# Moving the low weight halves by 64 bytes, and the first layer's mixer from three narrow products a block to a wide and a narrow one

## The chip, the cores and the metric

The kernel runs on one core of a Trainium2 chip. Its engines work side by side, each through a queue of its own: TensorE (PE; its weight loads are listed as PEld), VectorE (DVE), ScalarE (ACT), GpSimd (POOL) and SyncE (SP), which here issues the DMAs. The metric is the device time of one execution in microseconds.

## The reference

Two layers over one sequence of 256 tokens with 2,048 features, in float32. In each layer:

- from the vector `c`, 6 x 2,048 modulation values (a product with `ada_w`, 2,048 x 12,288);
- a root-mean-square norm of x with modulation, then one input projection `w_in` (2,048 x 8,704) into queries, keys and values of two attentions (A: a window of 128 tokens with grouped keys; B: a neighbourhood on a grid 64 wide, with a bias table) and two gates of 2,048 columns;
- each attention's output is projected (`w_proj_a`, `w_proj_b`, 1,024 x 2,048), multiplied by the sigmoid of its gate, and the sum goes through `w_out` (2,048 x 2,048) and is added to x;
- a second modulated norm, `w_up` (2,048 x 11,264), a depthwise convolution of width 3 over the tokens, SiLU of one half times the other half, `w_down` (5,632 x 2,048), added to x.

```
h = rmsnorm(x, norm_mix[l]) * (1.0 + sc_a) + sh_a
qa, ka, va, qb, kb, vb, ga, gb = split_cols(h @ w_in[l])
...
merged = jax.nn.sigmoid(ga) * ya + jax.nn.sigmoid(gb) * yb
x = x + gt_a * (merged @ w_out[l])
```

## The kernel before

**Blocks and units.** All weight matrices are cut into blocks of 128 x 128. A layer has 232 units of 16 blocks, in the order in which they are used (`block_stream`, L69). A unit is one DMA of 1 MB into a `raw` tile (four buffers, shared with the modulation weights `aw`, each 1 MB as well). `unit` (L216) splits each half of it, 8 blocks, into two float32r tiles: ScalarE copies the rounded value, *hi* (L225), and VectorE subtracts it from the original, *lo* (L226). Both lie in one tile `hl` of 128 x 2 x 1,024 elements, lo 4,096 bytes after hi in each partition; there are four such buffers, two units.

**Products.** The activations are split in the same way: `h[:, kc, 0]` is the high half, `h[:, kc, 1]` the low one, 256 tokens each, side by side. A product is the sum of three: hi with high, hi with low, lo with high.

- *Features* (`feature_run`, L230): a weight block stands in the array, the activations stream through. In the *joint* form there are three products of 256 columns a block, all into the same half of a PSUM bank (L239 to L241). In the other form there is a *wide* one of 512 columns, hi with both halves of the activations (L248 or L253), into both halves of the bank, and a *narrow* one of 256, lo with the high half (L250). A run has the blocks of half a unit: in a first run the wide products come first and then the narrow ones, in a later run the narrow ones and then the wide ones. The two halves of the bank have then to be added: `sum_halves` (L344) is a ScalarE copy of one (L346) and a VectorE addition of the other (L347).
- *Tokens* (`tokens`, L326): for queries, keys and values the activations stand in the array and four weight blocks stream (L337 to L339), 512 columns each.

**Stages of a layer**, in order: token products for q, k, v; gate A (`gate_a`); projection A (`proj_a`); gate B (`gate_b`); projection B (`merge`); out-projection (`out_evac`, with `residual`); then three times an up-projection with its convolution and a down-projection (`down`). Layer 0 works its token products and gate A in four parts of the contraction, with gate A always joint. `JOINT` (L49) says for proj_a, gate_b, merge and the out-projection whether they are joint: in layer 0 they are, in layer 1 not. `whole` (L738) gives the evacuation the bank's half where it is joint, and a tile `z` with the sum of halves where it isn't; `residual` (L782) takes one VectorE operation a column where joint, and two where not. The last column (from `ENDING` = 15) of an out-projection and of the last down-projection is joint in both layers.

**What sets the order.** The code is written in the order of the weight stream. Between units `Stream.tick` runs background work: `Paced` (L176) advances the attention heads by a rate a tick, and `plan` (L165) issues modulation products (L162, VectorE) so that a given number is done at a given unit (`ADA_PLAN_0`, `ADA_PLAN_1`); three quarters of them fall into layer 0. SP issues the DMAs in order and waits for a free `raw` buffer, which VectorE gives back. PSUM has four banks for these products (`mm`) and three for the rest (`ax`).

**Where the tiles lie.** Pools are laid out in the order in which they are made: `const` (with x), `lay`, `raw`, `hl`, `h` (h and merged share one place), `ev`, `at`, `sm`, and `s`, which holds ya, the packed q, k, v, oA, oB and the activations between up- and down-projection. oA's heads 6 and 7 lie in `ev`. In bytes of a partition: hl from 70,688, h from 103,456, ev's tiles for oA 6 and 7 from 140,320, s from 163,296; a tile's place is rounded up to 32 bytes.

Of the kernel before, what the change touches and what calls it, by code (L numbers as in the profile page):

```python
# [9 lines left out]
F32 = mybir.dt.float32  # L10
F32R = mybir.dt.float32r
AF = mybir.ActivationFunctionType
ALU = mybir.AluOpType
AX = mybir.AxisListType

P = 128
L = 2
# [16 lines left out]
GATE_A, GATE_B = 4608, 6656  # L34
# [11 lines left out]
ADA_PLAN_0 = [(38, 32), (58, 48), (76, 66), (84, 70), (96, 80), (128, 96), (145, 108), (175, 118), (192, 124), (230, 143)]  # L46
ADA_PLAN_1 = [(0, 143), (76, 169), (84, 165), (95, 176), (129, 192)]

JOINT = [True, False]  # L49

FIRST_RATE = 0.65
ENDING = 15
# [16 lines left out]
def block_stream(l):  # L69

    seq = []
    for part in K_PARTS[l]:
        for g in QKV_GROUPS:
            for kc in part:
                seq += [("w_in", kc, g // P + j) for j in range(4)]
        for mo in range(KC):
            seq += [("w_in", kc, GATE_A // P + mo) for kc in part]
    for mo in range(KC):
        seq += [("w_proj_a", kc, mo) for kc in range(HA)]
    for mo in range(KC):  # L80
        seq += [("w_in", kc, GATE_B // P + mo) for kc in range(KC)]
    for mo in range(KC):
        seq += [("w_proj_b", kc, mo) for kc in range(HB)]
    for mos in OUT_TURNS:
        seq += [("w_out", kc, mo) for kc in range(KC) for mo in mos]
    for gi, chunks in enumerate(FF_GROUPS):
        cols = [c + h * FC for c in chunks for h in range(2)]
        if gi == 0:
            for kc in range(KC):
                seq += [("w_up", kc, m) for m in cols[:4]]  # L90
            cols = cols[4:]
        for m in cols:
            seq += [("w_up", kc, m) for kc in range(KC)]
        for mos in OUT_TURNS:
            seq += [("w_down", kc, mo) for kc in chunks for mo in mos]
    return seq


UB = 16
NU = len(block_stream(0)) // UB  # L100
NA = len(ADA_ORDER)


# [1 line left out]
def encoder(ctx: ExitStack, tc: tile.TileContext, a: dict, out: bass.AP):  # L105
    nc = tc.nc
    pool = lambda name, bufs, **kw: ctx.enter_context(tc.tile_pool(name=name, bufs=bufs, **kw))
    const = pool("const", 1)
    lay = pool("lay", 2)
    rawp = pool("raw", 4)  # L110
    hlp = pool("hl", 4)
    hp = pool("h", 1)
    ev = pool("ev", 3)
    at = pool("at", 2)
    sm = pool("sm", 3)
# [19 lines left out]

    cact = const.tile([P, D], F32, name="cact")
    nc.sync.dma_start(cact[:1], a["c"])
    one = sm.tile([1, P], F32, name="one", tag="one", bufs=1)
    nc.vector.memset(one[:], 1.0)
    for i in range(0, D, 512):  # L140
        cb = ax.tile([P, 512], F32, name="cb", tag="ax")
        nc.tensor.matmul(cb[:], one[:], cact[:1, i : i + 512], start=True, stop=True)
        nc.scalar.activation(out=cact[:, i : i + 512], in_=cb[:], func=AF.Silu)
    x = const.tile([P, KC, S], F32, name="x")
    sp = pool("s", 1)

    def place(tag, n, dt, name):
# [67 lines left out]

    def unit(l, u):  # L216

        raw = rawp.tile([P, UB * P], F32, name=f"w{l}_{u}", tag="raw")
        nc.sync.dma_start(raw[:], a["ws"][l, u])
        halves = []  # L220
        for j in range(2):
            n = UB * P // 2
            hl = hlp.tile([P, 2, n], F32R, name=f"hl{l}_{u}_{j}", tag="hl")
            r = raw[:, j * n : (j + 1) * n]
            nc.scalar.copy(hl[:, 0], r)  # L225
            nc.vector.tensor_tensor(out=hl[:, 1], in0=r, in1=hl[:, 0].bitcast(F32), op=ALU.subtract)  # L226
            halves.append(hl)
        return halves

    def feature_run(run, joint):  # L230

        wide, narrow = [], []
        for ps, hl, j, act, first, last in run:
            hi, lo = hl[:, 0, j * P : (j + 1) * P], hl[:, 1, j * P : (j + 1) * P]
            out = ps[:].rearrange("p (a s) -> p a s", a=2)
            if joint:
                nc.tensor.matmul(out[:, 0], hi, act[:, 0], start=first, stop=False)  # L239
                nc.tensor.matmul(out[:, 0], hi, act[:, 1], start=False, stop=False)  # L240
                nc.tensor.matmul(out[:, 0], lo, act[:, 0], start=False, stop=last)  # L241
                continue
            wide.append((out, hi, act, first, last))
            narrow.append((out[:, 0], lo, act[:, 0]))
        begins = any(w[3] for w in wide)
        for o, w, act, first, last in wide:
            if begins and not last:
                nc.tensor.matmul(o, w, act, start=first, stop=False)  # L248
        for o, w, act in narrow:
            nc.tensor.matmul(o, w, act, start=False, stop=False)  # L250
        for o, w, act, first, last in wide:
            if last or not begins:
                nc.tensor.matmul(o, w, act, start=False, stop=last)  # L253

    class Stream:
# [16 lines left out]
        def prefetch(self, n):  # L272

            for _ in range(n):
                self.ahead.append(unit(self.l, self.u + len(self.ahead)))
# [13 lines left out]
        def next_block(self):  # L289
            if self.at == UB:  # L290
                if self.ahead:
                    self.halves = self.ahead.popleft()
                else:
                    with self.held():
                        self.halves = unit(self.l, self.u)
                self.u, self.at = self.u + 1, 0
            j = self.at
            self.at += 1
            return self.halves[j // 8], j % 8
# [26 lines left out]
        def tokens(self, h, kcs):  # L326

            pss = [mm.tile([P, 512], F32, name=f"ps{self.l}_{self.u}_t{t}", tag="mm") for t in range(2)]
            for kc in kcs:
                self.feed(kc)  # L330
                for _ in range(4):
                    hl, j = self.next_block()
                j -= 3
                hi, lo = hl[:, 0, j * P : (j + 4) * P], hl[:, 1, j * P : (j + 4) * P]
                for t, ps in enumerate(pss):
                    xh, xl = (h[:, kc, i, t * P : (t + 1) * P] for i in range(2))
                    nc.tensor.matmul(ps[:], xh, hi, start=kc == kcs[0], stop=False)  # L337
                    nc.tensor.matmul(ps[:], xh, lo, start=False, stop=False)  # L338
                    nc.tensor.matmul(ps[:], xl, hi, start=False, stop=kc == kcs[-1])  # L339
                if self.at == UB:  # L340
                    self.tick()
            return pss
# [259 lines left out]
    for l in range(L):  # L602
# [132 lines left out]

        joint = JOINT[l]

# [227 lines left out]
```

## Time and profile before

| what | us |
|---|---|
| three runs | 2775.48, 2775.0, 2773.64; median 2775.0 |
| the profiled execution | 2775.14, span 2773.4, granted TensorE clock 0.991 |
| busy: TensorE, VectorE, ScalarE | 2715.0, 2214.0, 1450.3 |
| weight split, lo (L226), 928 times | 1131.3 on VectorE, 1,223 ns each |
| weight split, hi (L225), 928 times | 972.5 on ScalarE, 1,050 ns each |
| modulation products (L162), 192 | 450.7 on VectorE, 2,347 ns each |
| out-projection, layer 0 and layer 1 | from 568.0 and from 1929.6 |
| first up-projection, layer 0 and layer 1 | from 671.1 and from 2029.9 |

A row of the profile's groups has the line, the engine, the operation, out<-in by the program's names, shape and count, then busy time and the mean duration of one. The duration of a matmul reaches from its issue to the modelled end of its pipeline; neighbours overlap. A row of the timeline begins with the start from the span's start and the time until the end of the last of the instructions merged in it.

### The profile page before, as it was taken

How to read it: one execution, taken by the hardware profiler on the slowest of the kernel's cores; microseconds unless marked ns; L12 is line 12 of the kernel's file. 1: busy time of each engine (PE TensorE's matmuls, PEld its weight loads, DVE VectorE, ACT ScalarE, POOL GpSimd, SP SyncE). 2: the span in 40 equal slices, each digit the busy share in tenths (PEclk: the TensorE clock that was granted, in tenths of full speed). 3: DMA queues.
4: the chain of work that ended last, by engine and by line, in shares of the span. 5: the costliest groups of instructions: out<-in, count | busy, mean ns of one | idle time of the engine just before them, and what ended most of it. 6: DMA issues, size and time to landing. Idle time of an engine off the chain costs nothing.

```text
span 2773.4 us, 39861 instructions
## 1 busy us (share of the span) xinstructions
PE 2715.0 (98%) x15930; PEld 2398.7 (86%) x15930; DVE 2214.0 (80%) x3163; ACT 1450.3 (52%) x2137; POOL 39.3 (1%) x24
## 2 busy tenths in 40 slices
PE   7899999999999999999999999999989999999999
PEld 5788799998888888888878888888878888888888
DVE  6998987897999888789976666768989767766775
ACT  5344684444654455355544567555455535544553
POOL 0000100000000000000000000000000000000000
PEclk9999999999999999999999999999999999999999
DMA  8887588896778766777756666665867655555553
GB/s 314 334 329 264 214 308 329 329 331 231 279 279 328 276 255 245 271 274 286 291 190 238 228 227 233 232 254 199 306 222 287 243 190 187 193 186 194 184 196 137
DMA packets 101852, 699.72 MB, mean 252 GB/s; under 512 B 12705, under 2 KB 15009, under 8 KB 17697
## 3 DMA queue, kind: packets, MB, share of 16 engines
q1 hardware_dynamic: 101666, 697.17, 68.2%
q8 instruction: 125, 2.05, 0.3%
q14 instruction: 61, 0.50, 0.1%
HBM read 695.03 MB, written 2.10 MB: 251 GB/s over the span
## 4 chain that ended last, share of the span: by engine, by line
PE 79%; issue 14%; DVE 4%; POOL 1%; ACT 1%; DMA 0%; POOLq 0%; SPq 0%; ACTq 0%; DVEq 0%
PE ps L253 20%; PE ps L250 18%; PE ps L248 15%; PE ps_t L338 4%; PE ps L240 4%; PE ps L239 4%; PE ps L241 4%; PE ps_t L339 4%; PE ps_t L337 4%; DVE aw L162 1%; DVE hl L226 1%; POOL qrs L390 1%; PE sc L485 1%; PE po L516 1%; ACT hl L225 0%
## 5 line engine op out<-in xcount | busy, mean ns | idle before, releaser
L226 DVE TENSOR_TENSOR hl<-w,hl 128x1024 fp32r<-128x1024 f32 x928 | 1131.3, 1223 | 307.6 <-ACT hl L225 300.8
L225 ACT CAST hl<-w 128x1024 fp32r<-128x1024 f32 x928 | 972.5, 1050 | 756.3 <-PE ps L253 174.5
L162 DVE CUSTOM_DVE_ANT_0 aw<-aw,cact,ab 128x2048 f32<-128x2048 f32 x192 | 450.7, 2347 | 25.5 <-DMA aw<-in_aw 25.1
L250 PEld LDWEIGHTS ps<-h,hl 128*128 128x128 f32 x3328 | 428.0, 191 | 16.9
L250 PE MATMUL ps<-h,hl 128*128 128x256 f32 x3328 | 432.9, 283 | 0.0
L253 PE MATMUL ps<-h,hl 128*128 128x512 f32 x1712 | 428.7, 392 | 0.0
L248 PE MATMUL ps<-h,hl 128*128 128x512 f32 x1616 | 406.4, 394 | 5.5 <-DVE cpad L347 4.5
L248 PEld LDWEIGHTS ps<-h,hl 128*128 128x128 f32 x1616 | 306.3, 190 | 70.8 <-DVE cpad L347 5.4
L253 PEld LDWEIGHTS ps<-h,hl 128*128 128x128 f32 x1712 | 307.9, 189 | 55.0
L346 ACT COPY r<-ps 128x256 f32<-128x256 f32 x240 | 88.9, 372 | 286.0 <-PE ps L253 286.0
L337 PE MATMUL ps_t<-hl,h 128*128 128x512 f32 x576 | 228.1, 401 | 7.5 <-ACT hl L225 7.0
L338 PE MATMUL ps_t<-hl,h 128*128 128x512 f32 x576 | 228.6, 397 | 4.7 <-DVE hl L226 4.7
L339 PE MATMUL ps_t<-hl,h 128*128 128x512 f32 x576 | 227.6, 396 | 0.9 <-DVE h L426 0.9
L826 DVE SCALAR_TENSOR_TENSOR u<-cpad,cw,u 128x256 f32<-128x256 f32 x352 | 168.7, 481 | 7.6 <-ACT u L824 3.2
L241 PE MATMUL ps<-h,hl 128*128 128x256 f32 x512 | 145.9, 285 | 0.0
L239 PE MATMUL ps<-h,hl 128*128 128x256 f32 x512 | 145.3, 284 | 0.0
L240 PE MATMUL ps<-h,hl 128*128 128x256 f32 x512 | 145.0, 283 | 0.0
L786 DVE SCALAR_TENSOR_TENSOR x<-ps,mod,x 128x256 f32<-128x256 f32 x237 | 111.5, 481 | 40.5 <-PE ps L253 30.4
L337 PEld LDWEIGHTS ps_t<-hl,h 128*128 128x128 f32 x576 | 109.8, 191 | 31.1 <-ACT hl L225 7.6
L338 PEld LDWEIGHTS ps_t<-hl,h 128*128 128x128 f32 x576 | 110.0, 191 | 30.8 <-DVE hl L226 8.1
L339 PEld LDWEIGHTS ps_t<-hl,h 128*128 128x128 f32 x576 | 109.9, 191 | 24.3 <-DVE h L426 1.4
L347 DVE TENSOR_TENSOR cpad<-ps,r 128x256 f32<-128x256 f32 x176 | 74.4, 424 | 63.2 <-ACT r L346 63.0
(202 smaller groups left out, 3610.4 us busy)
## 6 DMA issues: line engine op xcount, KB each, us to landing
w<-in_ws SPq DMA_DIRECT2D x464, 1024.0 KB, 4.9
aw<-in_aw SPq DMA_DIRECT2D x192, 1024.0 KB, 4.9
bias<-in_bias SPq DMA_DIRECT2D x16, 256.0 KB, 4.4
x<-in_xT SPq DMA_DIRECT2D x4, 512.0 KB, 5.6
out<-x SPq DMA_DIRECT2D x16, 128.0 KB, 1.8
cw<-in_cw SPq DMA_DIRECT2D x2, 176.0 KB, 4.0
maskA<-in_maskA SPq DMA_DIRECT2D x1, 256.0 KB, 5.3
ab<-in_ab SPq DMA_DIRECT2D x2, 48.0 KB, 7.1
```

The lines of the kernel that those rows point to most:

```text
L162: nc.vector.tensor_tensor_reduce(out=raw[:], in0=raw[:], in1=cact[:], scale=1.0, scalar=ab[:, i : i + 1], op0=ALU.mult, op1=ALU.add, accum ...
L225: nc.scalar.copy(hl[:, 0], r)
L226: nc.vector.tensor_tensor(out=hl[:, 1], in0=r, in1=hl[:, 0].bitcast(F32), op=ALU.subtract)
L239: nc.tensor.matmul(out[:, 0], hi, act[:, 0], start=first, stop=False)
L240: nc.tensor.matmul(out[:, 0], hi, act[:, 1], start=False, stop=False)
L241: nc.tensor.matmul(out[:, 0], lo, act[:, 0], start=False, stop=last)
L248: nc.tensor.matmul(o, w, act, start=first, stop=False)
L250: nc.tensor.matmul(o, w, act, start=False, stop=False)
L253: nc.tensor.matmul(o, w, act, start=False, stop=last)
L337: nc.tensor.matmul(ps[:], xh, hi, start=kc == kcs[0], stop=False)
L338: nc.tensor.matmul(ps[:], xh, lo, start=False, stop=False)
L339: nc.tensor.matmul(ps[:], xl, hi, start=False, stop=kc == kcs[-1])
```

## The change

Three things are done at once.

1. The tile `hl` gets 32 more elements (128 bytes). hi begins 16 elements (64 bytes) into it. lo follows hi directly where the unit holds blocks for the token products (`streamed`), and 64 bytes further elsewhere. The products read the two halves by views and are otherwise the same.
2. Two pads of 64 bytes are laid between pools, one ahead of `h` and one ahead of `s`; VectorE clears each once at the start. The small tile `one` of the start goes to a place of the pool `at`, which gives 512 bytes back.
3. `JOINT` is false for layer 0 too: its proj_a, gate_b, merge and out-projection (but for the last column) use wide and narrow products with sums of halves.

```diff
-JOINT = [True, False]
+JOINT = [False, False]
...
+ROW = 32
+STREAMS = [block_stream(l) for l in range(L)]
...
+    skips = []
+
+    def skip(n):
+
+        skips.append(pool(f"skip{len(skips)}", 1).tile([P, n // 4], F32, name=f"skip{len(skips)}"))
+        nc.vector.memset(skips[-1][:], 0.0)
+
     const = pool("const", 1)
     lay = pool("lay", 2)
     rawp = pool("raw", 4)
     hlp = pool("hl", 4)
+    skip(64)
     hp = pool("h", 1)
...
-    one = sm.tile([1, P], F32, name="one", tag="one", bufs=1)
+    one = at.tile([1, P], F32, name="one", tag="qsq", bufs=1)
...
     x = const.tile([P, KC, S], F32, name="x")
+    skip(64)
     sp = pool("s", 1)
...
         halves = []
+        streamed = any(m == "w_in" and mo < GATE_A // P for m, _, mo in STREAMS[l][u * UB : (u + 1) * UB])
         for j in range(2):
             n = UB * P // 2
-            hl = hlp.tile([P, 2, n], F32R, name=f"hl{l}_{u}_{j}", tag="hl")
+            hl = hlp.tile([P, 2 * n + ROW], F32R, name=f"hl{l}_{u}_{j}", tag="hl")
+            at = ROW // 2 + n + (0 if streamed else ROW // 2)
+            hi, lo = hl[:, ROW // 2 : ROW // 2 + n], hl[:, at : at + n]
             r = raw[:, j * n : (j + 1) * n]
-            nc.scalar.copy(hl[:, 0], r)
-            nc.vector.tensor_tensor(out=hl[:, 1], in0=r, in1=hl[:, 0].bitcast(F32), op=ALU.subtract)
-            halves.append(hl)
+            nc.scalar.copy(hi, r)
+            nc.vector.tensor_tensor(out=lo, in0=r, in1=hi.bitcast(F32), op=ALU.subtract)
+            halves.append((hi, lo))
         return halves
...
-            hi, lo = hl[:, 0, j * P : (j + 1) * P], hl[:, 1, j * P : (j + 1) * P]
+            hi, lo = (w[:, j * P : (j + 1) * P] for w in hl)
...
-                hi, lo = hl[:, 0, j * P : (j + 4) * P], hl[:, 1, j * P : (j + 4) * P]
+                hi, lo = (w[:, j * P : (j + 4) * P] for w in hl)
```

## Prediction

> **What bounds the kernel now.** I read the page first, then the timeline of TensorE in four places, then the windows by stage. On the page TensorE is busy 98% of the span and no other engine is past 80%:
>
> ```profile
> span 2773.4 us, 39861 instructions
> PE 2715.0 (98%) x15930; PEld 2398.7 (86%) x15930; DVE 2214.0 (80%) x3163; ACT 1450.3 (52%) x2137; POOL 39.3 (1%) x24
> L250 PE MATMUL ps<-h,hl 128*128 128x256 f32 x3328 | 432.9, 283 | 0.0
> ```
>
> The 283 ns is the latency of one matmul; they are pipelined, so what counts is the distance between starts. The timeline gives it. First one unit (16 blocks) of the up-projection, where the moving operand is h; then one unit of a down-projection, where it is act; then layer 0's out-projection on merged and its B projection on oB, both in three 256-wide products per block.
>
> ```profile
> 1004.71 1.98 PE L248 MATMUL ps<-h,hl 128*128 128x512 f32 x8
> 1006.52 2.08 PE L250 MATMUL ps<-h,hl 128*128 128x256 f32 x16
> 1008.43 2.00 PE L253 MATMUL ps<-h,hl 128*128 128x512 f32 x8
> 1010.27 1.98 PE L248 MATMUL ps<-h,hl 128*128 128x512 f32 x8
> ```
> ```profile
> 2502.40 2.03 PE L248 MATMUL ps<-act_b,hl 128*128 128x512 f32 x8
> 2504.26 1.53 PE L250 MATMUL ps<-act_b,hl 128*128 128x256 f32 x12
> 2505.63 0.62 PE L250 MATMUL ps<-act_y,hl 128*128 128x256 f32 x4
> 2506.08 1.09 PE L253 MATMUL ps<-act_b,hl 128*128 128x512 f32 x4
> 2507.01 1.10 PE L253 MATMUL ps<-act_y,hl 128*128 128x512 f32 x4
> 2507.94 2.03 PE L248 MATMUL ps<-act_b,hl 128*128 128x512 f32 x8
> ```
> ```profile
> 600.07 0.28 PE L239 MATMUL ps<-merged,hl 128*128 128x256 f32 x1
> 600.43 0.28 PE L239 MATMUL ps<-merged,hl 128*128 128x256 f32 x1
> 540.17 0.28 PE L239 MATMUL ps<-oB,hl 128*128 128x256 f32 x1
> 540.51 0.28 PE L239 MATMUL ps<-oB,hl 128*128 128x256 f32 x1
> ```
>
> Differences of starts: with h, eight wide products take 1.81 us (L248) or 1.84 (L253) and sixteen narrow ones 1.91. With act the wide eights take 1.86 and the sixteen narrow ones 1.82. A joint block takes 0.36 us on merged and 0.34 on oB. So the same instruction takes 119 or 113.5 ns (narrow) and 226 or 232 ns (wide), by which tile it reads, whatever ScalarE and VectorE do beside it (the spacing is the same over rows with a weight split, a modulation product or nothing beside them).
>
> The tiles differ in their place. Four hl tiles of 8,192 bytes lie in a row and h (and merged) follows them directly, so h lies a whole multiple of 128 bytes from every hi and lo. The pool s (act, oB, oA 0 to 5) begins 92,608 bytes after the first hl, 64 bytes off a multiple of 128. A second case of this inside one tile family: oA 6 and 7 lie in the pool ev, 69,632 bytes after hl, a multiple of 128. Where the joint products of layer 0 run from oA 5 to oA 6, their spacing goes from 113 to 114 ns up to 117 to 121. So, in rows: equal places make wide products fast and narrow ones slow, 64 bytes off the reverse. No place of today gives both.
>
> The windows by stage (layer 0: proj_a, gate_b, proj_b, out; layer 1: proj_a, proj_b) say what else is near its limit there. Columns: window, its length, then busy us of each engine, granted clock, DMA share, GB/s.
>
> ```profile
> 371.00:432.40 61.40, 61.33 (x471) 58.54 (x470) 52.84 (x102) 41.76 (x80) 0.00 (x0) 1.00 0.84 301
> 432.40:524.50 92.10, 92.10 (x769) 92.10 (x769) 71.92 (x69) 38.72 (x48) 0.00 (x0) 1.00 0.92 347
> 524.50:568.00 43.50, 43.50 (x386) 43.50 (x385) 41.73 (x69) 22.10 (x31) 0.00 (x0) 1.00 0.78 289
> 568.00:663.00 95.00, 92.56 (x772) 92.36 (x771) 79.79 (x99) 40.86 (x52) 0.00 (x0) 1.00 0.88 322
> 1746.80:1795.90 49.10, 49.10 (x282) 42.83 (x281) 40.50 (x70) 27.13 (x51) 0.00 (x0) 1.00 0.64 233
> 1885.20:1929.60 44.40, 44.40 (x258) 38.69 (x257) 41.63 (x76) 27.59 (x48) 0.00 (x0) 1.00 0.52 189
> ```
>
> **The change, part by part.** The sum is made against the profiled execution, 2775.14 us (span 2773.4 and 1.7 around it); it lies 0.1 us above the median of 2775.0, so nothing is corrected.
>
> Places afterwards, from the tile sizes: an hl tile has 8,320 bytes (65 x 128), hi starts 64 bytes in, h moves by 4 x 128 + 64, the pool s by 64 more (its 512 bytes from hl are given back by `one`). So h, merged and all acts lie a multiple of 128 from every hi, and 64 off every lo, except in units with token blocks, where lo keeps hi's place. Wide products then stand as h's do today, narrow ones as act's. The best of the two rows above is 1.81 + 1.81 + 1.81, about 5.44 us a unit.
>
> *Units on h and merged, wide and narrow today.* 3,328 + 240 blocks are 223 units; 5.56 to 5.44, so 0.12 x 223 = 26.8 us.
>
> *Units on act, and layer 1's oA and oB.* 1,638 blocks, 102 units; 5.54 to 5.44: 10.2 us.
>
> *Layer 0 no longer joint.* gate_b has 16 units, out 15 (the last column stays joint): 16 x 0.36 = 5.76 to 5.44, 0.32 x 31 = 9.9 us. The two projections: 0.34 to 0.34 a block, nothing.
>
> *Layer 0's gate_a stays joint.* In its order hi, hi, lo one of three weight loads now lies 64 off: between 0 and 0.32 a unit over 16 units. I take 0.1 and half of that, since VectorE is 97% busy around two of its four pieces: 0.8 us.
>
> *Token products.* hi, lo and h keep their relation in 128: nothing. Bounds below, under the rivals.
>
> Sum of the gains: 47.7 us. TensorE has no wait in these stages outside the norms, so they count in full but for what follows.
>
> *Changing between runs.* No row shows a narrow run 64 off behind a wide run in place. Today a narrow run on act begins with one at 118 (5 ns lost), one on h with none lost; a wide run in place behind h's narrow run loses 27 ns over its first five (233, 236, 228, 232, 231, against 227), one on act begins at 226 (nothing lost). I take 5 ns for the first, as its products are act's, and for the second 8 of 0 to 27, as the run left behind is act's but the phase to be found is h's. On 372 units (5,958 blocks wide and narrow): 1.8 + 3.0 = 4.8 us; ends 0 and 12.
>
> *Layer 0's evacuations.* 48 sums of halves (copy 372 ns on ScalarE, add 424 on VectorE, starts about 335 apart) and 15 second residual products (481; starts 395 apart): 16 + 6 = 22 us on VectorE, 16 to 18 on ScalarE. In proj_a VectorE goes from 52.8 to 58 of 61.4 us, and the ScalarE copy now waits for a bank in front of queued weight casts and the attention's exponentials, for which TensorE waits in turn; layer 1 has the same work in its 49.1 us with almost no wait. I take 2 us. In proj_b VectorE would need 41.7 + 5.4 = 47.1 of 43.5 us; four banks and two units of split weights (some 10 us) cover most of the 3.6, and out has to take it over with 79.8 + 5.9 of about 90 us; if that cover fails the 3.6 shows. I take 2. In gate_b the transfers are at a share of 0.92; 92.1 us less 5.1 puts them at 0.97, so the weights may come late, and the sigmoid now waits for VectorE's add with the next casts queued behind it: 2 of the 5.1. Together 6; ends 0 and 22 (all of VectorE's new work).
>
> *The rest.* Two memsets of 16 columns at the start lie beside the loads of c and x; `one` in the place of qsq is written 270 us before the first qsq: nothing. The splits' own time is left as it is, 1,223 and 1,050 ns: their destinations move by 64 or 128 bytes, and no row shows a split that depends on it.
>
> Sum: 47.7 - 4.8 - 6 = 36.9, so 2775.1 - 36.9 = **2738 us**.
>
> One rule speaks against all but the joint part. The Trainium skill, "TensorE: Matmul & The Clock Gate", section on what each phase is for, says that TensorE has two independent read ports and that loading the next weights takes no read bandwidth from the running matmul; "SBUF — State Buffer", section on its two separate sides, allows contention only between VectorE and GpSimd. By that rule the first two terms, 37 us, would be nothing and the time about 2775. The trace disagrees: 119 against 113.5 ns for one and the same shape.
>
> **The rivals.**
>
> *The place is not the cause, the tile is.* Then only layer 0 gains: its units go from 5.76 to h's 5.56, 0.20 x 31 = 6.2 us, and the 6 us of evacuations eat it: 2775. For it: each tile has one place in the trace. Against it: oA changes its spacing between its own heads.
>
> *The narrow products settle in another phase.* After a stall the joint products on oA 0 to 5 run at 117 to 118 for a whole column instead of 113, and layer 1's narrow ones on oA too. If all of the 5,958 do: 4.35 ns each, 26 us, less the 1.8 charged already: 2762. Against it: act and layer 1's oB, 1,510 narrow products, come back to 113 after one.
>
> *Layer 0 has no room.* All 22 us of VectorE's work show instead of 6: 2754. For it: 96% in proj_b, 0.92 of the transfers in gate_b. Against it: no wait of TensorE in either stage.
>
> *The pattern repeats at 256 or 512 bytes, not at 128.* The rows exclude neither: today all distances are multiples of 512, or 64 off one. Blocks lie 512 apart and all of a run go alike, so it is not over 512. The new hl tiles stand 128 apart in it. At 512 three of the four are off for the wide products: 4,064 wide on h and merged (gate_b and out included) and 3,456 token products lose 6.25 ns each in three cases of four, 19.0 + 16.2, and three quarters of act's 10.2 do not come, 7.6. With the phase to be found anew at each tile, the 27 ns in place of 8 for each unit's wide run in place cost some 5: 36.9 - 42.8 - 5 = -11, so **2786**, slower. At 256 half of the tiles are off: 36.9 - 28.5, 2767. It decides where more than two of four tiles are off.
>
> **How the numbers follow.** Forecast 0.58; layer 0 without room 0.10; narrow products in the other phase 0.12; repeat at 256, 0.06; at 512, 0.07; tile and not place 0.07. A measurement here tells about 0.2%, 5.5 us, from no change. Faster by more: the first four, 0.86; within: 0.06; slower: 0.08, the repeat at 512 and a part of the tile's case. The forecast's own range is 2726 to 2750 (the ends of the phase and evacuation terms that can go together). To leave out no more than 2 in 10, the range reaches to the other phase and the repeat at 256: 2722 to 2767.
>
> **What would show it.** Narrow starts 113 to 114 ns apart on h and merged; wide ones 226 to 227 on act; units of 5.44 to 5.48 us in the up- and down-projections of both layers; token products unchanged at 227; gate_b near 87 us and out's 15 columns near 82. Wrong: narrow starts at 118 on h; wide or token starts that change from one half unit to the next (the repeat); waits of TensorE for hl in gate_b or for a bank in proj_b; VectorE at 100% from proj_a to out.

## The result and the profile after

The changed kernel takes 2779.8 us (median of 20 runs, 2776.8 to 2781.6), the kernel before 2773.7 in the runs beside them (20 runs, 2771.0 to 2778.1). The ratio is 1.0018, with a 95% interval of 1.0012 to 1.0025: slower by a little, where 2738 us was forecast. The profiled execution took 2780.7 us; its page:

```profile
span 2778.7 us, 38471 instructions
PE 2713.7 (98%) x15178; PEld 2355.1 (85%) x15178; DVE 2236.7 (80%) x3228; ACT 1464.4 (53%) x2185; POOL 39.3 (1%) x24
L268 PE MATMUL ps<-h,hl 128*128 128x256 f32 x3584 | 458.0, 280 | 0.0
```

752 blocks of layer 0 take two products instead of three, and TensorE is busy as long as before. The mean of a narrow product went from 283 to 280 ns, which is a latency and shows nothing; the starts do. TensorE's timeline over one unit of an up-projection of layer 1 and the next start (start, time to the end, then the group):

```profile
2312.41 2.02 PE L266 MATMUL ps<-h,hl 128*128 128x512 f32 x8
2314.27 2.03 PE L268 MATMUL ps<-h,hl 128*128 128x256 f32 x16
2316.14 2.01 PE L271 MATMUL ps<-h,hl 128*128 128x512 f32 x8
2317.98 2.02 PE L266 MATMUL ps<-h,hl 128*128 128x512 f32 x8
```

The unit takes 5.57 us, as before (5.56), in other parts: the first eight wide products now 1.86, the sixteen narrow ones 1.87 and the second wide ones 1.84. Forecast were 1.81 each. Inside the narrow run the two half units differ: the first eight products start mostly 117 to 119 ns apart, the other eight 117, 122 and 119 and then 113 to 114. In layer 0 the parts are 1.82, 1.88 and 1.86. So the two `hl` tiles of a unit no longer stand alike.

To add this up over the kernel, I took from both traces every distance between two starts. What a product takes over 226.7 ns (512 columns) or 113.35 ns (256 columns), the best that the traces show, is called *excess* below; where it is over some 16 ns, TensorE waited for something or ran at a lower granted clock, and it is counted under *waits*.

| us | excess before | excess after | waits before | waits after |
|---|---|---|---|---|
| token products, both layers | 0.9 | 6.2 | 34.8 | 32.6 |
| layer 0, gate_a | 4.9 | 3.3 | 3.0 | 3.2 |
| layer 0, proj_a and proj_b | 0.9 | 2.0 | 3.6 | 4.0 |
| layer 0, gate_b and out | 10.2 | 3.8 | 3.0 | 10.5 |
| layer 1, gate_a to out | 8.6 | 8.2 | 5.0 | 5.0 |
| up-projections | 22.4 | 21.5 | 10.6 | 11.0 |
| down-projections | 9.6 | 11.2 | 3.8 | 3.8 |
| all | 57.4 | 56.4 | 63.7 | 70.1 |

The excess fell by 1.0 and the waits rose by 6.4 us: together 5.4 us, where the span grew by 5.3 (2773.4 to 2778.7). Nearly all of the new wait is in one place. Windows of layer 0's proj_a, gate_b, proj_b and out in the changed kernel (columns as in the prediction), then TensorE's timeline at the change from proj_b to out, its waits around it (total us, times, longest), and below them the one wait of the kernel before that is its counterpart:

```profile
371.50:433.00 61.50, 61.23 (x341) 52.09 (x340) 57.22 (x115) 45.00 (x94) 0.00 (x0) 1.00 0.80 289
433.00:522.60 89.60, 89.60 (x516) 78.78 (x516) 75.70 (x85) 42.70 (x64) 0.00 (x0) 1.00 0.96 354
522.60:567.30 44.70, 44.70 (x257) 39.08 (x256) 43.39 (x79) 27.34 (x47) 0.00 (x0) 1.00 0.70 252
567.30:662.00 94.70, 90.50 (x531) 79.65 (x529) 87.54 (x116) 40.53 (x51) 0.00 (x0) 0.98 0.88 323
```
```profile
567.96 0.62 PE L266 MATMUL ps<-merged,hl 128*128 128x512 f32 x2
...
572.65 1.67 PE L268 MATMUL ps<-merged,hl 128*128 128x256 f32 x8 [4.06 <-DVE hl L244]
```
```profile
PE ps L268 <- DVE hl L244: 4.1, 1, 4.1
PE ssm L397 <- DVE sqa L389: 3.9, 1, 3.9
```
```profile
PE ssm L379 <- DVE sqa L371: 2.7, 1, 2.7
```

VectorE is busy 97% of proj_b (43.39 of 44.70), and the first narrow product of out waits 4.1 us for its low weights, which VectorE writes too late. The norm's squares at the end of out (L389) are late by 3.9 us, 2.7 before; VectorE is busy for 87.5 of out's 94.7 us.

The two waits are not all of it. Behind the first one TensorE has a lower granted clock for a while (the column ahead of the DMA share):

```profile
572.60:576.50 3.90, 3.71 (x17) 3.42 (x18) 3.90 (x6) 1.46 (x2) 0.00 (x0) 0.58 0.53 181
```

The eight narrow products that start at 572.65 take 1.67 us there, 0.21 each. By the starts, out's 10.5 us (3.0 before) are 4.2 for the late weights, 2.2 for products at the lower clock behind them, and 4.1 for the squares (2.9 before).

### The profile page after: what moved, and what is told of

Its sections match the earlier page's. It is cut to its first block, busy times and chain, and to the rows that moved or that the text cites. A ratio compares the mean times of both kernels' runs of the same rounds, so it can differ in the third digit from the quotient of the medians.

```text
span 2778.7 us, 38471 instructions
## 1 busy us (share of the span) xinstructions
PE 2713.7 (98%) x15178; PEld 2355.1 (85%) x15178; DVE 2236.7 (80%) x3228; ACT 1464.4 (53%) x2185; POOL 39.3 (1%) x24
## 4 chain that ended last, share of the span: by engine, by line
PE 78%; issue 14%; DVE 5%; ACT 1%; POOL 1%; DMA 1%; POOLq 0%; SPq 0%; ACTq 0%; DVEq 0%
PE ps L271 22%; PE ps L268 21%; PE ps L266 19%; PE ps_t L356 4%; PE ps_t L357 4%; PE ps_t L355 4%; DVE aw L174 1%; DVE hl L244 1%; PE ps L259 1%; PE ps L258 1%; PE ps L257 1%; POOL qrs L408 1%; PE sc L503 1%; PE po L534 1%; ACT hl L243 0%
## 5 line engine op out<-in xcount | busy, mean ns | idle before, releaser
L268 PEld LDWEIGHTS ps<-h,hl 128*128 128x128 f32 x3584 | 454.5, 189 | 19.0
L271 PE MATMUL ps<-h,hl 128*128 128x512 f32 x1840 | 463.4, 394 | 0.0
L268 PE MATMUL ps<-h,hl 128*128 128x256 f32 x3584 | 458.0, 280 | 0.0
L266 PE MATMUL ps<-h,hl 128*128 128x512 f32 x1744 | 442.8, 396 | 5.5 <-DVE cpad L365 4.5
L266 PEld LDWEIGHTS ps<-h,hl 128*128 128x128 f32 x1744 | 330.5, 190 | 80.6 <-DVE cpad L365 5.4
L271 PEld LDWEIGHTS ps<-h,hl 128*128 128x128 f32 x1840 | 329.5, 188 | 60.3
L364 ACT COPY r<-ps 128x256 f32<-128x256 f32 x288 | 106.6, 372 | 322.3 <-PE ps L271 322.0
L804 DVE SCALAR_TENSOR_TENSOR x<-ps,mod,x 128x256 f32<-128x256 f32 x252 | 118.3, 480 | 44.1 <-PE ps L271 34.7
L842 ACT ACTIVATE u<-cpad,cw 128x256 f32<-128x256 f32 x176 | 105.5, 601 | 15.0 <-DVE cpad L365 14.8
L271 PE MATMUL ps<-act_a,hl 128*128 128x512 f32 x342 | 93.5, 393 | 0.0
L259 PE MATMUL ps<-h,hl 128*128 128x256 f32 x256 | 72.8, 285 | 0.0
```

Source lines behind the costliest of these rows:

```text
L364: nc.scalar.copy(r[:], ps[:, S:])
L804: nc.vector.scalar_tensor_tensor(out=x[:, mo], in0=ps[:, half], scalar=gt, in1=x[:, mo], op0=ALU.mult, op1=ALU.add)
```

## The experiments

Two theories stood after the result. *Repeat at 256*: what counts is the distance in bytes, by its remainder at 256, from the weights that are being loaded to the operand that streams; tiles of 8,320 bytes stand at 0 and 128 by turns. *Tile, not place*: the spacing belongs to the buffer and its use, and the excess would not follow the places. Beside these: how much of the loss is layer 0's new VectorE work, and why narrow products did not go at 113. A distance below is that of the streaming operand less the weight loaded meanwhile, modulo 256; "in place" is 0.

**The stride of the tiles.** The changed kernel with `hl` tiles of 8,448 bytes (33 x 256).

```diff
-            hl = hlp.tile([P, 2 * n + ROW], F32R, name=f"hl{l}_{u}_{j}", tag="hl")
+            hl = hlp.tile([P, 2 * n + 2 * ROW], F32R, name=f"hl{l}_{u}_{j}", tag="hl")
...
-        rg = load(a["rg"][l], [P, 2, ROT], f"rg{l}", lay, tag="rg")
+        rg = load(a["rg"][l], [P, 2, ROT], f"rg{l}", lay, tag="rg", bufs=1)
```

> The changed kernel with hl tiles of 8,448 bytes (33 x 256) in place of 8,320, so that all four lie alike to 256 bytes (a table of layer 1 gets one buffer instead of two to make room). Theory R (the pattern repeats at 256 bytes, and the changed kernel fails because its four tiles alternate between two places): wide starts 227 ns and narrow ones 113 to 114 apart on h and act, token products back at 227; the excess of the matmul spacing over 226.7 and 113.35 ns falls from 56 us to about 10, so 2780 - 45 = about 2735 us. Theory P (the phase found behind a run in place is the 118 ns one, whatever the tiles do): narrow starts at 117 to 118 everywhere, wide at 227: about 2760. Theory E (layer 0's added evacuations are what costs): no change, 2778 to 2780.

Measured: 2767.6 us (2764.4 to 2770.4), ratio to the kernel before 0.9976 (0.9968 to 0.9985). TensorE's timeline over the same kind of unit:

```profile
2302.36 1.98 PE L266 MATMUL ps<-h,hl 128*128 128x512 f32 x8
2304.17 2.05 PE L268 MATMUL ps<-h,hl 128*128 128x256 f32 x16
2306.06 2.00 PE L271 MATMUL ps<-h,hl 128*128 128x512 f32 x8
2307.90 1.98 PE L266 MATMUL ps<-h,hl 128*128 128x512 f32 x8
```

The first wide run is back at 1.81 (226.7 ns steadily, where it was 229 to 241 at a distance of 128) and token products at 227 (excess 6.2 to 1.1). But the unit is 5.54 and not 5.44: the narrow run takes 1.89 (117.7 ns), and the wide run behind it starts with 234, 235, 229, 232, 231 before it is at 227. The time lies in none of the three ranges: the wide and token products came as Theory R had them, the narrow ones as Theory P had them. The repeat at 256 stands; it is worth 12 us of the 42 between forecast and result.

**Each part alone.** The changed kernel with layer 0 joint again; the kernel before with layer 0 not joint; and the tiles of 8,448 bytes with layer 0 joint.

```diff
-JOINT = [False, False]
+JOINT = [True, False]
```

> The changed kernel with layer 0 joint again: the new places alone. Theory R: the places alone bring nothing here, as the tiles alternate (excess of the spacing 56 to 60 us as before the change): layer 0 gives back the 6.4 us gained in gate_b and the out-projection and gets back the 7.5 us of waits, so 2777 to 2780, still 4 us over the kernel before, from the token products (5 us). Theory E: the loss goes with the evacuations, 2765 to 2772.

```diff
-JOINT = [True, False]
+JOINT = [False, False]
```

> The kernel before with layer 0 wide and narrow and the old places: the evacuations alone. The 31 units of gate_b and the out-projection go from 5.76 to 5.56 us, 6 us gained; the waits at the beginning of the out-projection cost 5 to 8. Theory R: 2772 to 2776, as before. Theory E: 2778 to 2781, all of the loss.

> Places alike to 256 bytes in all tiles, as in the first of these runs, and layer 0 joint again. Theory R: the gain of the places without layer 0's new work: narrow starts 113 to 114 on h and act outside layer 0's mixer; gate_b and the out-projection of layer 0 stay at 117 to 120 ns a product (up to 10 us lost against the first run), the 7.5 us of waits are gone: 2730 to 2738. Theory P: about 2760. Theory E: 2765 to 2772.

| | us | ratio to before | excess | waits |
|---|---|---|---|---|
| places as changed, layer 0 joint | 2773.9 | 1.0001 (0.9992 to 1.0010) | 58.4 | 63.3 |
| old places, layer 0 not joint | 2777.0 | 1.0012 (1.0003 to 1.0021) | 52.3 | 76.6 |
| 8,448 bytes, layer 0 joint | 2765.5 | 0.9968 (0.9957 to 0.9979) | 49.0 | 63.1 |

The places as they were changed are worth nothing by themselves. Leaving the joint form lowers the excess (57.4 to 52.3; in gate_b and out from 10.2 to 4.2) and lengthens the waits by more: out of layer 0 waits 12.3 us in the second row and 3.0 in the others. The execution profiled for that row was the longest of its runs (2781.6), so that its sums are some 4.5 us larger than its median; the granted clock behind its late weights is 0.57 for longer (from 573.6 to 581.5).

The times alone would not have decided: 2773.9 and 2777.0 lie between the ranges of the theories R and E, and 2765.5 falls into that of E, though layer 0's form is worth only 2.1 us on these tiles (2767.6 to 2765.5). It is the excess and the waits that tell the parts from each other.

**Other distances for lo.** On the 8,448-byte tiles with layer 0 joint, lo 128 or 192 bytes further than hi's end instead of 64.

```diff
-            at = ROW // 2 + n + (0 if streamed else ROW // 2)
+            at = ROW // 2 + n + (0 if streamed else ROW)
```

> All tiles alike to 256 bytes and layer 0 joint, but lo 128 bytes off hi in place of 64. Theory P (the spacing of a run comes from the distance modulo 256 and from the phase that the run before leaves): wide starts stay at 227 in their steady state, narrow ones settle elsewhere than at 117.6; 113.4 would be 20 to 24 us off the 2765.5 of the run with 64 bytes (about 2743), 120 would be 10 us on it (about 2776). Theory R (the distance modulo 256 alone, with 0 and 128 alike as both halves of a bank): 119 to 120, about 2775.

```diff
-            at = ROW // 2 + n + (0 if streamed else ROW // 2)
+            at = ROW // 2 + n + (0 if streamed else 3 * ROW // 2)
```

> The same with lo 192 bytes off hi. Theory P: another settled spacing of the narrow products than at 64 and 128 bytes is possible, between 113 (2743) and 120 (2776); the half units of the changed kernel that stood so were at 117.6 behind mixed neighbours, so 117 to 118 and 2763 to 2768 is the likeliest. Theory R: 64 and 192 alike, 117.6, 2765.

Measured: 2778.4 (ratio 1.0013, 1.0003 to 1.0023) with narrow products at 120.2 ns, and 2774.9 (1.0003, 0.9994 to 1.0012) with 117.8 and the second wide run at 232.8. Of the three, 64 bytes is the best, and none brings 113.

**Place or tile.** The kernel before with a gap of 64 bytes ahead of h. So h stands 64 off the weights, and the activations, which were 64 off on the other side (192 by the remainder), stand in place.

```diff
     hlp = pool("hl", 4)
+    gap = pool("gap", 1).tile([P, 16], F32, name="gap")
+    nc.vector.memset(gap[:], 0.0)
     hp = pool("h", 1)
```

> The kernel before with one gap of 64 bytes between hl and h, so that h stands 64 off hi and lo and the acts stand in place: the two families change their sides, and h's distance has the other sign than act's had. If the place alone counts: narrow 113 to 114 and wide 231 to 234 on h, narrow 120 and wide 227 on act; on h 3,568 narrow products gain 6 ns and 3,568 wide ones and 3,456 token products lose 5 to 6, in all 2780 to 2795 us. If the tile and not its place counts: no change, 2774. If the sign counts: narrow on h at 117 to 118.

Measured: 2773.0 us in one run, 7 us below the range expected if the place counts. Its timeline over a unit of a down-projection:

```profile
2506.38 1.98 PE L250 MATMUL ps<-act_b,hl 128*128 128x512 f32 x8
2508.19 1.59 PE L252 MATMUL ps<-act_b,hl 128*128 128x256 f32 x12
2509.63 0.64 PE L252 MATMUL ps<-act_y,hl 128*128 128x256 f32 x4
2510.11 1.09 PE L255 MATMUL ps<-act_b,hl 128*128 128x512 f32 x4
2511.04 1.07 PE L255 MATMUL ps<-act_y,hl 128*128 128x512 f32 x4
2511.95 1.98 PE L250 MATMUL ps<-act_b,hl 128*128 128x512 f32 x8
```

The activations have taken over h's old numbers to within a hundredth: 1.81, then 1.92 for the narrow run, then 1.84 (before: 1.86, 1.82, 1.86). Tile, not place, is refuted. On h, at a distance of 64, the wide starts went to 226, 229 and 232 ns by turns (229.3 in the mean), and its narrow runs were at 113 to 114 in half of the cases and at 117 to 118 in the other half: one distance, two spacings. The time is below the range as the wide products on h lost 0.7 ns each (228.6 before) and not 5 to 6, and as the range counted 3,456 token products where the trace has 1,728. Two neighbouring units of an up-projection:

```profile
2312.86 2.00 PE L250 MATMUL ps<-h,hl 128*128 128x512 f32 x8
2314.70 1.98 PE L252 MATMUL ps<-h,hl 128*128 128x256 f32 x16
2316.51 1.99 PE L255 MATMUL ps<-h,hl 128*128 128x512 f32 x8
2318.34 1.99 PE L250 MATMUL ps<-h,hl 128*128 128x512 f32 x8
2320.17 2.05 PE L252 MATMUL ps<-h,hl 128*128 128x256 f32 x16
2322.05 2.00 PE L255 MATMUL ps<-h,hl 128*128 128x512 f32 x8
2323.89 2.00 PE L250 MATMUL ps<-h,hl 128*128 128x512 f32 x8
```

The narrow runs take 1.81 and 1.88, the units 5.48 and 5.55: the first is what was hoped for, at a distance that the change did not aim at. What comes ahead differs by a few ns. Over all such runs on h and merged, the last wide product took 231 or 232 ns ahead of each of the 111 narrow runs at 113, and 230 or less ahead of 117 of the 120 at 118. So the spacing goes with the step of the pattern at which the wide run ends; that the step causes it is not tested.

The token products agree with the distance and its sign. There the weights stream and the activations are loaded, so that h at 64 is a distance of 192 for them: 233.4 ns. In the run with h at 192, further down, it is 64: 229.2.

By the rule of the Trainium skill weighed in the prediction ("TensorE: Matmul & The Clock Gate", section on what each phase is for), loading weights takes nothing from the running product; the same instruction on act at 113 ns before and 120 here, by its place against the weights loaded beside it, disagrees.

The same with a gap of 128 bytes (`[P, 32]`):

> The kernel before with a gap of 128 bytes between hl and h: h 128 off, act 64 off with the other sign. A pattern of 128 bytes: nothing changes, narrow 120 and wide 227 on h, 2774 us. A pattern of 256 bytes: h's wide products go to 229 to 238 and its token products too, 2785 to 2800.

Measured: 2790.9 us in one run, excess 75.6. Wide and token products at a distance of 128 take 232.6 ns, narrow ones 118.7. A repeat at 128 would have left h's numbers as they were. It is refuted.

**A shorter product at the border.** To see what sets the narrow run's spacing, the last wide product ahead of each narrow run was cut into two of 256 columns (on the 8,448-byte tiles, layer 0 joint); then the first wide one behind it too.

```diff
-        for o, w, act, first, last in wide:
-            if begins and not last:
+        early = [w for w in wide if begins and not w[4]]
+        for k, (o, w, act, first, last) in enumerate(early):
+            if k == len(early) - 1 and not first:
+                for half in range(2):
+                    nc.tensor.matmul(o[:, half], w, act[:, half], start=False, stop=False)
+            else:
                 nc.tensor.matmul(o, w, act, start=first, stop=False)
```

> All tiles alike to 256 bytes, layer 0 joint (2765.5 us in its run), and the last wide product ahead of each narrow run made as two products of 256 columns: the same sum, another phase at the entry of the narrow run. Theory P (the narrow products 64 off have two settled spacings, 113.4 and 117.6, and the entry chooses): narrow starts at 113 to 114 behind the split; 4,950 of them gain 4.3 ns, 21 us, and some 310 splits cost 7 to 14 ns each, 2 to 4 us, so about 2748. Theory D (the distance alone sets the spacing): 117.6 stays and the splits are paid, 2768 to 2770.

```diff
         for o, w, act, first, last in wide:
-            if last or not begins:
+            if (last or not begins) and not last and w is wide[0][1]:
+                for half in range(2):
+                    nc.tensor.matmul(o[:, half], w, act[:, half], start=False, stop=False)
+            elif last or not begins:
```

> The same, and the first wide product behind a narrow run split as well. Theory P: the 27 ns that a wide run in place loses over its first five products behind a narrow run shrink to 5 to 15, less 7 to 14 for the split: within 3 us of the run with one split, on either side. Theory D: another 2 to 4 us slower than it.

Measured: 2770.6 (0.9984, 0.9974 to 0.9993) and 2774.9 (1.0001, 0.9991 to 1.0010), against 2765.5 without the cuts. Narrow products stay at 117.7 to 117.9 ns. A single short product does not change the spacing, and only costs.

**Wide and narrow by turns.** In the same kernel, each block's wide and narrow product one behind the other instead of in runs of eight. Then hi is loaded while a narrow product streams, and lo while a wide one does. In the second version hi and lo have changed places (outside the units with token blocks).

```diff
...
+        for (o, w, act, first, last), (no, nw, nact) in zip(wide, narrow):
+            if last:
+                nc.tensor.matmul(no, nw, nact, start=False, stop=False)
+            nc.tensor.matmul(o, w, act, start=first, stop=last)
+            if not last:
+                nc.tensor.matmul(no, nw, nact, start=False, stop=False)
```

> All tiles alike to 256 bytes, layer 0 joint, and in the other stages the wide and the narrow product of a block one behind the other, in place of runs of eight. The reading that what counts is the distance between the operand that streams and the weights that are loaded meanwhile: a wide product now has lo loading, 64 off, and a narrow one hi, in place: 231 to 233 and 119 to 120, 351 ns a block against 345 in runs, 6 ns on some 4,950 blocks, 30 us: about 2795. If the distance to the product's own weights counted instead, as in runs: 344, 2762.

```diff
             hi, lo = hl[:, ROW // 2 : ROW // 2 + n], hl[:, at : at + n]
+            if not streamed:
+                hi, lo = lo, hi
```

> The same with hi and lo changed over outside the token units: lo in place, hi 64 off. The weights loaded meanwhile count: wide 227 and narrow 113 to 118, 340 to 345 a block: 2738 to 2763. The product's own weights count: wide 231 to 233 and narrow 120, 352 a block, about 2797.

Measured: 2790.1 (1.0057, 1.0042 to 1.0072), with wide products at 235.1 and narrow ones at 117.3; and 2768.8 (0.9978, 0.9969 to 0.9988), with 231.4 and 117.2. In the first, the wide products' own weights stand in place and the weights loaded meanwhile at 192; in the second it is the other way round. The order of the products is the same, and the wide ones are 4 ns slower in the first. So the weights loaded meanwhile count, not the own ones. In the second these are in place, and the wide ones are still at 231 and not at 227: a steady stretch of one kind is needed as well. Its time is some 6 us above the range expected.

**Bytes, or the run ahead.** Two runs for why narrow products at 192 take 113.4 on act in the kernel before, and 117.7 on the 8,448-byte tiles. First, those tiles (layer 0 joint) with 128 bytes ahead of `hl`, which gives lo and the streaming operand the same absolute places modulo 256 as lo and act before. Second, the kernel before with h at 192, where a narrow run has the distance and the places of the 8,448-byte kernel without this gap, but the wide run ahead of it stands at 192 too instead of in place (act then stands at 128).

```diff
     rawp = pool("raw", 4)
+    gap0 = pool("gap0", 1).tile([P, 32], F32, name="gap0")
+    nc.vector.memset(gap0[:], 0.0)
     hlp = pool("hl", 4)
```

> All tiles alike to 256 bytes, layer 0 joint (2765.5 us in its run), and everything from the raw buffers on moved by 128 bytes, so that lo and the moving half stand at the same bytes modulo 256 as lo and act did before the change, where narrow starts were at 113.4. If the bytes themselves count and not only the distance: narrow 113 to 114, about 2744. If the run ahead counts (a wide run in place leaves the narrow one at 117.6): no change, 117.6 and 2763 to 2768.

```diff
     rawp = pool("raw", 4)
+    gap0 = pool("gap0", 1).tile([P, 32], F32, name="gap0")
+    nc.vector.memset(gap0[:], 0.0)
     hlp = pool("hl", 4)
+    gap1 = pool("gap1", 1).tile([P, 48], F32, name="gap1")
+    nc.vector.memset(gap1[:], 0.0)
     hp = pool("h", 1)
```

> The kernel before with all moved by 128 bytes and h by 192 more. The narrow products on h then stand at the same bytes and the same distance as in the kernels with tiles alike to 256, but the wide products ahead of them are 64 off instead of in place. If the run ahead counts: narrow 113 to 114 on h, wide 231 to 236 in turns, as act had it. If the bytes count: narrow 117 to 118. Its time tells nothing: h's wide and token products lose 3 to 6 ns each, 2780 to 2795.

Measured: 2763.6 (0.9961, 0.9946 to 0.9976), and 2765.8 in one run, 14 us below the range that was expected of it. The timelines of the two, one unit each:

```profile
2303.72 1.98 PE L268 MATMUL ps<-h,hl 128*128 128x512 f32 x8
2305.53 2.05 PE L270 MATMUL ps<-h,hl 128*128 128x256 f32 x16
2307.42 2.00 PE L273 MATMUL ps<-h,hl 128*128 128x512 f32 x8
```
```profile
2302.94 2.03 PE L252 MATMUL ps<-h,hl 128*128 128x512 f32 x8
2304.80 1.98 PE L254 MATMUL ps<-h,hl 128*128 128x256 f32 x16
2306.62 2.02 PE L257 MATMUL ps<-h,hl 128*128 128x512 f32 x8
2308.48 2.03 PE L252 MATMUL ps<-h,hl 128*128 128x512 f32 x8
```

The absolute places change nothing: 1.81 and 1.89 as without the gap. The run ahead does: behind a wide run at 192 (1.86) the narrow run at 192 takes 1.82, and starts some 113 ns apart after its first. Both units are 5.54 us. At these places one kind of run pays for the other; the 1.81 of all three parts was a sum of rows that no trace here shows together. No unit of wide and narrow runs is below 5.47 us in any trace, and all those below 5.50 stand at a distance of 64, 100 of them with h there (above). The run ahead is not all either. Layer 0's joint products of this run, with h and merged in one place, start 113.3 ns apart in gate_b and 117.5 in out.

**The evacuations.** The 8,448-byte tiles with gate_b and out of layer 0 wide and narrow, and its two projections joint.

```diff
-        def whole(ps):
+        def whole(ps, joint=joint):
...
-                nc.vector.tensor_tensor(out=ya[:, mo], in0=whole(ps), in1=ya[:, mo], op=ALU.mult)
+                nc.vector.tensor_tensor(out=ya[:, mo], in0=whole(ps, l == 0), in1=ya[:, mo], op=ALU.mult)
...
-            st.features(oA, [proj_a], joint=joint)
+            st.features(oA, [proj_a], joint=l == 0)
...
-                nc.vector.tensor_tensor(out=z[:], in0=whole(ps), in1=gb[mo], op=ALU.mult)
+                nc.vector.tensor_tensor(out=z[:], in0=whole(ps, l == 0), in1=gb[mo], op=ALU.mult)
...
-            st.features(oB, [merge], joint=joint)
+            st.features(oB, [merge], joint=l == 0)
```

> All tiles alike to 256 bytes; in layer 0 gate_b and the out-projection wide and narrow, the two projections joint. If the waits of 7 to 8 us at the beginning of the out-projection come from the sums of halves in proj_b, which VectorE has no room for: they go, and the two stages keep what they gained, 3 us: 2761 to 2764. If they come from the second residual products of the out-projection or from gate_b: they stay, about 2768.

Measured: 2760.5 (0.9951, 0.9937 to 0.9966), 7.1 us below the same with wide and narrow projections. Its waits of TensorE from proj_b to the end of out:

```profile
PE ssm L397 <- DVE sqa L389: 2.7, 1, 2.7
PE rb L427 <- POOL nrs L421: 1.8, 1, 1.8
```

The wait for hl is gone and the squares are at 2.7 again; out of layer 0 waits 3.0 us instead of 11.2, although its 15 second residual products are still there. The waits come from the sums of halves in the projections.

**All joint.** Joint products showed 113.4 ns at a distance of 192 (in proj_b before, and in gate_b of the run with h at 192). So: all feature products joint in both layers (a block is then three narrow products, with no wide run ahead), hi and lo both 64 bytes off (the distance is 192 to both), token units in place, no sums of halves but a ScalarE copy in the convolution. The form of the up- and down-projections is set the same way where they are called, and two small tiles (rg, rot) have one buffer to make room.

```diff
-JOINT = [False, False]
+JOINT = [True, True]
...
-    skip(64)
+    skip(192)
     hp = pool("h", 1)
...
-            at = ROW // 2 + n + (0 if streamed else ROW // 2)
-            hi, lo = hl[:, ROW // 2 : ROW // 2 + n], hl[:, at : at + n]
+            at = 3 * ROW // 2 if streamed else 0
+            hi, lo = hl[:, at : at + n], hl[:, at + n : at + 2 * n]
...
-            sum_halves(ps, pad[:, 1 : S + 1])
+            nc.scalar.copy(pad[:, 1 : S + 1], ps[:, :S])
```

> Every feature product joint (three of 256 columns a block, in both layers and in the feed-forward too, so that no sum of halves is left), all activations 64 bytes off hi and lo as act and oB were before the change, token units in place. Joint products at that distance were at 113.4 ns on oB before and on h in gate_b of the run with the other entry, and at 117.6 on merged there. If they settle at 113.4 throughout: 5.44 us a unit in place of 5.54 to 5.56, about 35 us off the kernel before, 2735 to 2745. If they settle at 117.6: 5.64 us a unit, 2785 to 2800. In turns, by the stall ahead of each stage: between.

Measured: 2739.9 us as the median of four runs that lie far apart (2726.7 to 2756.1), ratio 0.9866 (0.9814 to 0.9919): the best of all, and faster than both kernels. Every third start (the first product of a block) in two places of its timeline, the first two lines' blocks being on h and the last three's on act:

```profile
799.95 0.28 PE L257 MATMUL ps<-h,hl 128*128 128x256 f32 x1
...
800.29 0.28 PE L257 MATMUL ps<-h,hl 128*128 128x256 f32 x1
...
899.81 0.28 PE L257 MATMUL ps<-act_o,hl 128*128 128x256 f32 x1
...
900.17 0.28 PE L257 MATMUL ps<-act_o,hl 128*128 128x256 f32 x1
...
900.52 0.28 PE L257 MATMUL ps<-act_o,hl 128*128 128x256 f32 x1
```

Three products take 0.34 us in the one place and 0.35 to 0.36 in the other. The distance is the same throughout. Over the trace the spacing is 113.3 ns for whole stretches (675 to 850 us, 2025 to 2725) and 117.8 for others (425 to 650, 875 to 1400, 1800 to 2000); it changes only where a stage changes, where TensorE has waited or where other products stand between. Layer 1's up-projections take 479.9 us with no excess, layer 0's, with the same code and places, 492.5 with 12.3. Which of the two a stretch falls into could explain why the times spread over 29 us; that is not shown, as there is no trace of the other three executions.

## Why the prediction was wrong

The terms as they were forecast, as the changed kernel has them, and as the 8,448-byte tiles have them (us against before, from the excess and waits of the traces; minus is faster):

| term | forecast | changed kernel | 8,448 bytes |
|---|---|---|---|
| units on h, merged, act, layer 1's oA and oB, with what is lost between runs | -37.0 + 4.8 | +0.3 | -6.5 |
| layer 0's gate_b and out no longer joint | -9.9 | -6.4 | -7.0 |
| layer 0's projections | 0 | +1.1 | +0.8 |
| layer 0's gate_a | -0.8 | -1.6 | -1.2 |
| token products | 0 | +5.3 | +0.2 |
| evacuations and all other waits | +6 | +6.4 | +7.6 |

- **"Places afterwards": failed.** The step took a multiple of 128 bytes for "in place". The pattern repeats at 256, and `hl` tiles 8,320 bytes apart stand at 0 and 128 by turns. By the four tiles in turn, layer 1's token products in the changed kernel start 232.4, 228.2, 232.4 and 228.1 ns apart: neighbours differ, every second tile agrees, which excludes 128 and 512. The rival that said so had a chance of 0.06 and was priced at 2767; the result is 13 us above, since the price was subtracted from a gain that isn't there. The price itself was too high: it counts 3,456 token products, and the trace has 1,728 (576 on each of three lines). By its own sum it is then 23 us and not 28.5, and the time 2761.
- **"The best of the two rows is 1.81 + 1.81 + 1.81": failed.** This is the larger part. With the tiles alike, a unit is 1.81 + 1.89 + 1.84: narrow products settle at 117.7 behind a wide run in place. That was the rival of the other phase (0.12); its 2762 lies 5.6 us below what the 8,448-byte tiles took. Act's 113.4 had been read as a property of its distance. The run with h at 192 shows that the distance alone does not give it: at the same distance and places narrow products take 113.4 behind a wide run at 192.
- **"Changing between runs": too low.** Of 0 to 27 ns for a wide run in place behind a narrow one, 8 were taken. In the runs with 8,448-byte tiles and narrow products 192 off, such a run loses all 27 (1.84 for 1.81), on h and on act. With lo 128 bytes further it loses less on h (1.82), with lo 192 bytes further more (1.87).
- **"Token products: nothing": failed** with the first step. They read the same tiles, and lose 5.3 us at 128 (227 to 232 ns on half of the tiles).
- **Layer 0 no longer joint: right in kind.** 9.9 us forecast, 6.4 measured: the units that it went to are 5.56 and not 5.44.
- **Layer 0's evacuations: right in place, and in size partly by luck.** 6 us forecast; 7.5 more in out and 0.4 in the projections. They show where proj_b hands its backlog to out, as feared there, and go with joint projections. But 2 us were set for this hand-over, and it cost 4.2 with 2.2 more at the lower granted clock, for which the prediction has no term, and 1.2 more for the squares. The 2 us for gate_b did not come: it has no wait, though its transfers are at a share of 0.96.
- **Tile, not place: refuted**, by the gap of 64 bytes.

What stays open is why TensorE has two spacings at one distance. It goes with the run ahead (the run with h at 192) and, with h at 64, with the step at which that run ends; but the all-joint kernel has both without any wide run, a short product at the border does not switch it, and no profile line names what does. A kernel with the feature operands 64 off and the token units in place, where the shortest units were, has not been run.

## What to carry to other kernels

Where a tuned product differs in spacing between tiles, work out the distances for every buffer of a rotating pool, by remainders up to the largest period that the rows do not exclude: a stride that is right for one buffer can be wrong for the next. Two best rows from two neighbourhoods don't add up to a best unit until one trace shows them next to each other; the run ahead is part of the condition. And work that goes to VectorE in a stage where it is at 96% can come back as a late weight split in the next stage, even if the stage itself shows no wait. Such a wait can cost more than its own length: here 4.2 us were followed by 2.2 at a lower granted clock.

## What was not expected of the hardware

- The distance between starts of a float32r product depends on the place of the operand that streams against the weights that are loaded meanwhile, with a period of 256 bytes. In runs of one kind, 512 columns: 226.7 to 228 ns at 0, 226 to 232 at 64, 231 to 233 at 128, 231 and 236 by turns at 192. 256 columns: 119 to 120 at 0, 113.4 or 117.7 at 64, 118.7 or 120.2 at 128, 113.4 or 117.7 at 192.
- At one distance there can be two steady spacings, 113.3 and 117.7 to 117.8 ns for 256 columns. They change with the run ahead, a change of stage or a wait, and one can last for 700 us: the all-joint kernel varies by 29 us from run to run, the kernel before by 7.
- Behind a narrow run that is 192 off or in place, products of 512 columns in place need five of their kind (233, 236, 228, 233 and 231 ns in the mean) before they are at 227.
- Behind a wait of 4.2 us the granted clock of TensorE was 0.58 in the mean of the next 3.9 us, and eight products of 256 columns took 1.67 us.
